# A hybrid decoder block on one core: V and output gate of the linear attention in one product, accumulators kept in one set of pools, and the order of the last norms

## The chip, the cores and the metric

The kernel runs on one core of a Trainium2 chip. The metric is the device time in microseconds, the median over runs; before the change it is 1220.12 us (three runs, 1219.98 to 1223.33). Beside the runs there is one profiled execution, from which all rows below come.

## The reference

One layer over 512 tokens of width 1024, batch 1, all float32:

```
h = rms_norm(x, g0);  proj = h @ w_in                       # 10816 columns
y_a = rglru_mixer(lru_x, lru_g, ...)                        # conv of width 4, gates, linear recurrence
y_b = nsa_mixer(q, kv, gate, ...)                           # compressed, selected and window attention
y_c = gla_mixer(q, k, v, og, lr, ...)                       # 4 heads, keys of 128, values of 256, chunks of 32
merged = sum_i sigmoid(merge_i) * (y_i @ w_branch[i])
x = x + rms_norm(merged @ w_out, g1)
h = rms_norm(x, g2);  gt, up = split(h @ w_ffn_in)
x = x + rms_norm((silu(gt) * up) @ w_ffn_out, g3)
```

In `gla_mixer` each head does `o = causal(q_t k_t^T) v + q_t state`, the state runs over the sequence, and the output is `rms_norm(o) * silu(og)`.

## The kernel before

Every large product is made of three matmuls of two-part operands: each weight piece (128 partitions x 1024 values, from one or two transfers into `wraw`) is split into a high part `whi` (ACT casts, line 91) and a low part `wlo` (DVE or POOL subtracts, line 92), the activations are held as `hh` and `hl`, and high x high, high x low and low x high add up in one accumulator. `wraw`, `whi` and `wlo` have three buffers each. From the attention's end on the pieces are a list, in the order of their use, and `take` (line 815) splits two pieces ahead of the one that it hands out.

The program's stages, in order: first norm; the small projection and the compressed blocks (to about 95 us); the attention, with the other projections fed in between its parts (to 321); four LRU blocks (to 466); four heads of the linear attention (to 640); the merge (to 806); w_out and two norms (to 870); FFN's first product (to 1101); FFN's second product, last norm and store.

Up to the attention the framework's scheduler orders the work, by its own estimate of times. In the stages under `manual_schedule`, among them the attention, the LRU, the linear attention, the merge, and FFN's second product, each engine's queue is in the order in which the code issues it, so an instruction that waits holds up all behind it on its engine. Transfers of weights are issued from SP's queue, the sums that prepare FFN's second product from POOL's.

PSUM has eight banks. The attention uses four pools: `pg` (1), `pa` (4), `pt` (2), `po` (1). At its end these close and new ones open: `pg` with four banks, `pa` with two, `pt` with two. At FFN's second product they close again, and eight accumulators take all banks.

A head of the linear attention (line 1163) issues: the product for q and k (`stream_t`: weights stationary, 512 columns moving, two accumulators); `gla_qk` on DVE, which reads both accumulators and scales q and k by the decays; the transposes of the head before (`gla_turn`); V's product (`stream_tok`: activations stationary, 256 columns of weights moving, four row blocks in two accumulators); `gla_scores`; the output gate's product in the same form, and after it the exponentials for the next head; `gla_out` with the state (three products, three DVE operations), the Silu of the gate, the output, its squares and the root. `lru_params` (line 893) loads `wr`, splits it on ACT and DVE and computes the LRU's constants; it is issued ahead of the first LRU block. The last block's `lru_root` and `lru_scan` stand ahead of the first head.

FFN's second product is a product of 2 x 2 blocks with seven products p1 to p7 in place of eight. Its first loop makes p2, p5, p3 and p1 over eleven slices, then p4, p6 and p7 follow, each with five full weight pieces and a half one. `gain` squares half a row on ACT with its sum and multiplies it with the norm's weights on DVE in place, so the multiply waits for the square; `mean` and `root` make the row's factor, `store` multiplies, adds the residual and sends it off.

## Time and profile before

| | us |
|---|---|
| runs, median (lowest to highest) | 1220.12 (1219.98 to 1223.33) |
| profiled execution | 1221.34 |
| its span, first to last instruction | 1219.6 |
| TensorE busy | 1197.8 (98%) |
| DVE busy | 656.9 (54%) |
| ACT busy | 550.7 (45%) |
| POOL busy | 202.9 (17%) |

Busy time is the time in which an engine has at least one instruction under way. Matmuls overlap, so a recorded duration is longer than the time that a matmul takes from the next one. The view of waits lists for an engine who ended its idle times.

### The profile page before, as it was taken

Reading aid. Unit: us, or ns where it says so; the run is one execution under the profiler, and the core shown is the slowest. Engines: PE = TensorE matmul, PEld = TensorE weight load, DVE = VectorE, ACT = ScalarE, POOL = GpSimd, SP = SyncE. Lnnn points to the kernel's source line nnn. Section 1 sums busy time; section 2 is a strip of 40 time slices with the busy share of each in tenths; the row PEclk is TensorE's granted clock in tenths of the full one; section 3 lists DMA queues with packets and bytes.
Section 4 is the critical chain, followed back from the end, with each engine's and each line's share of the span. In section 5 each row is a group of like instructions: output and inputs, shape, how many; then the busy total and the mean of one; then the engine's idle time right before and its main releaser. Section 6 shows DMA issues by size and latency. Waiting matters only on the chain.

```text
span 1219.6 us, 18072 instructions
## 1 busy us (share of the span) xinstructions
PE 1197.8 (98%) x6834; PEld 1011.7 (83%) x6834; DVE 656.9 (54%) x1308; ACT 550.7 (45%) x1038; POOL 202.9 (17%) x261
## 2 busy tenths in 40 slices
PE   8999999999999999999999999999999999999995
PEld 7897888888788888999998888887988888887884
DVE  5615555555576779465543353446543433446786
ACT  5326556655387676443442233234432323324553
POOL 1224555665101113112221000000000000000000
PEclk8999999999999999999999999999999999999999
DMA  7831422221234547476669334244333333324652
GB/s 248 237 86 29 96 74 66 66 66 53 64 109 130 166 123 228 150 177 145 138 134 207 104 99 160 87 155 138 95 113 87 103 91 100 104 82 159 212 182 91
DMA packets 162102, 151.04 MB, mean 124 GB/s; under 512 B 26706, under 2 KB 139582, under 8 KB 161840
## 3 DMA queue, kind: packets, MB, share of 16 engines
q1 hardware_dynamic: 154912, 125.77, 34.9%
q0 software_dynamic: 6512, 23.07, 8.4%
q8 instruction: 54, 0.88, 0.3%
q10 hardware_dynamic: 592, 1.05, 0.2%
q14 instruction: 32, 0.26, 0.1%
HBM read 145.60 MB, written 27.34 MB: 142 GB/s over the span
## 4 chain that ended last, share of the span: by engine, by line
PE 92%; DVE 4%; ACT 2%; DMA 1%; issue 1%; SPq 0%; DVEq 0%; ACTq 0%
PE gps L836 17%; PE gps L164 14%; PE gps L839 9%; PE gps L122 8%; PE gps L123 7%; PE gps L124 7%; PE gps L167 7%; PE ops L668 4%; PE s L600 3%; PE ptp L646 3%; PE acc L123 3%; PE acc L122 3%; PE acc L124 3%; PE hid L434 1%; PE ops L1125 1%
## 5 line engine op out<-in xcount | busy, mean ns | idle before, releaser
L91 ACT CAST whi<-wraw 128x1024 fp32r<-128x1024 f32 x153 | 159.6, 1049 | 252.2 <-issue 100.7
L92 DVE TENSOR_TENSOR wlo<-wraw,whi 128x1024 fp32r<-128x1024 f32 x131 | 159.9, 1228 | 149.9 <-ACT whi L91 117.9
L164 PE MATMUL gps<-hh,whi 128*128 128x512 f32 x368 | 143.5, 390 | 0.0
L167 PE MATMUL gps<-hl,whi 128*128 128x512 f32 x368 | 143.4, 390 | 0.0
L836 PE MATMUL gps<-hh,whi 128*128 128x512 f32 x320 | 125.4, 392 | 1.6 <-ACT whi L91 1.6
L839 PE MATMUL gps<-hl,whi 128*128 128x512 f32 x320 | 124.6, 389 | 0.0
L122 PE MATMUL gps<-whi,hh 128*128 128x256 f32 x320 | 92.4, 289 | 0.0
L123 PE MATMUL gps<-wlo,hh 128*128 128x256 f32 x320 | 90.6, 283 | 1.4 <-DVE wlo L92 1.4
L164 PE MATMUL gps<-hh,wlo 128*128 128x512 f32 x368 | 90.9, 389 | 0.0
L124 PE MATMUL gps<-whi,hl 128*128 128x256 f32 x320 | 90.5, 283 | 0.0
L164 PEld LDWEIGHTS gps<-hh,whi 128*128 128x128 f32 x368 | 69.1, 188 | 15.0 <-issue 0.9
L167 PEld LDWEIGHTS gps<-hl,whi 128*128 128x128 f32 x368 | 69.1, 188 | 14.5 <-issue 0.2
L164 PEld LDWEIGHTS gps<-hh,wlo 128*128 128x128 f32 x368 | 69.1, 188 | 14.4
L650 DVE COPY psb<-ptp 128x512 f32<-128x512 f32 (+2 forms) x72 | 45.5, 631 | 65.3 <-PE ptp L646 61.6
L611 ACT ACTIVATE p<-p,mx 128x384 f32<-128x384 f32 (+3 forms) x128 | 68.7, 538 | 26.0 <-DVE mx L609 25.9
L836 PE MATMUL gps<-hh,wlo 128*128 128x512 f32 x320 | 79.1, 389 | 0.0
L625 POOL TENSOR_TENSOR p<-p,sc 128x256 f32<-128x256 f32 (+3 forms) x64 | 75.5, 1201 | 1.9
L808 POOL COPY tick<-whi 128x1 f32<-128x1 f32 x44 | 28.0, 636 | 284.2 <-ACT whi L91 284.1
L836 PE MATMUL gps<-yh,whi 128*128 128x512 f32 x192 | 74.8, 390 | 0.0
L839 PE MATMUL gps<-yl,whi 128*128 128x512 f32 x192 | 74.7, 389 | 0.0
L122 PE MATMUL gps<-hh,whi 128*128 128x512 f32 (+1 forms) x176 | 73.8, 420 | 0.1
L836 PEld LDWEIGHTS gps<-hh,whi 128*128 128x128 f32 x320 | 60.1, 188 | 14.5 <-ACT whi L91 2.0
(362 smaller groups left out, 2556.6 us busy)
## 6 DMA issues: line engine op xcount, KB each, us to landing
wraw<-in_w_in_dram SPq DMA_DIRECT2D x60, 512.0 KB, 4.1
wraw<-in_w_ffn_in_dram SPq DMA_DIRECT2D x88, 256.0 KB, 3.2
rows_d<-in_w_ffn_out_dram POOLq DMA_DIRECT2D x22, 512.0 KB, 5.2
cols_d<-in_w_ffn_out_dram POOLq DMA_DIRECT2D x22, 512.0 KB, 6.5
wraw<-in_w_in_dram SPq DMA_DIRECT2D x32, 256.0 KB, 4.1
wraw<-in_w_branch_dram SPq DMA_DIRECT2D x16, 512.0 KB, 3.4
wraw<-in_w_ffn_out_dram SPq DMA_DIRECT2D x18, 256.0 KB, 3.5
bias<-line_d SPq DMA_DIRECT2D x16, 256.0 KB, 4.5
```

The costliest lines, as they stand in the source:

```text
L91: a_.copy(hi, raw)
L92: lo_eng.tensor_tensor(lo, raw, f(hi), op=OP.subtract)
L122: pe.matmul(ps, lh, rh, start=first, stop=False)
L123: pe.matmul(ps, lh, rl, start=False, stop=False)
L124: pe.matmul(ps, ll, rh, start=False, stop=last)
L164: pe.matmul(ps[n], part_[:, k, c], ah[:, kk], start=kk == 0 and part_ is h, stop=kk == 7 and part_ is l)
L167: pe.matmul(ps[n], h[:, k, c], al[:, kk], start=False, stop=False)
L611: a_.activation(o, o, AF.Exp, scale=-1.0, bias=mx[:, br, gi:gi + 1], accum_out=sm[:, br, gi:gi + 1])
L625: g_.tensor_tensor(o, o, sc[:, br][:, :, None].to_broadcast([128, 2, n]), op=OP.mult)
L668: pe.matmul(ops[h, qb * 128:qb * 128 + 128], v, m, start=first and i == 0, stop=last and i == len(blocks) - 1)
L836: pe.matmul(ps[n], part_[:, k, c], ah[:, kk], start=kk == 0 and part_ is h, stop=kk == 7 and part_ is l)
L839: pe.matmul(ps[n], h[:, k, c], al[:, kk], start=False, stop=False)
```

## The change

Eight things are changed.

1. The product of V and the product of the output gate of one head become one product of 512 columns (`stream_vog` with pieces from `vog_pieces`: 256 rows of 256 + 256 columns, two transfers each, four pieces a head as before). It has four accumulators, one for each row block of 128 tokens; for the first two pieces two row blocks go first and then the other two. V is copied and the gate's Silu taken from these accumulators, by row block.
2. State and output of a head move into the next one: `gla_state` and the next head's exponentials stand between the two halves of the next q/k product, `gla_out` and `gla_gate` behind `gla_qk`, `gla_turn` behind the third piece of the next V and gate product. For the last head these places are in the merge's first chunk. `qs` gets a second buffer.
3. The last LRU block's `lru_root` and `lru_scan` stand between the halves of the first q/k product, the constants and the first exponentials behind it.
4. `lru_params` goes from ahead of the first LRU block to behind its gate products; the transfer of `wr` stays ahead.
5. In `small_proj` the reversed copy, four small products and the gates' sigmoid go ahead of the low-rank part.
6. The attention's PSUM pools stay to the end: `Banks` hands out the four banks of the old `pa` as the new `pg`, and those of `pg` and `po` in turn as the new `pa`. FFN's second product takes its eight accumulators from them.
7. In FFN's second product the additions of p1 come two pieces later, the gains of the second halves of blocks 0 and 1 move from p4 into p6, `gain` writes to another tile for one half of each block, the last half-width weight piece is loaded and split during p6 into a place of its own, and roots and stores of the last blocks are issued in another order.
8. A Sqrt of one constant column is issued on ACT behind the last FFN chunk.

The diff, cut to its core:

```diff
+        gps = pt.tile([128, TB, 64], F32, name="gtps", tag="pt")
+        srev = pp.tile([128, TB, 128], F32, name="srev", tag="psb", bufs=NPSB)
+        v_.tensor_copy(srev, sps.rearrange("p (b c) -> p b c", b=TB)[:, :, ::-1])
+        for tb in range(TB):
+            pe.matmul(gps[:, tb], srev[:, tb], ii, start=True, stop=True)
+        a_.activation(gates, gps[:, :, 16:64], AF.Sigmoid)
...
-        gps = pt.tile([128, TB, 64], F32, name="gtps", tag="pt")
-        srev = pp.tile([128, TB, 128], F32, name="srev", tag="psb", bufs=NPSB)
-        v_.tensor_copy(srev, sps.rearrange("p (b c) -> p b c", b=TB)[:, :, ::-1])
-        for tb in range(TB):
-            pe.matmul(gps[:, tb], srev[:, tb], ii, start=True, stop=True)
-        a_.activation(gates, gps[:, :, 16:64], AF.Sigmoid)
...
-    psum_ctx.close()
-    psum_ctx = ExitStack()
-    pg = psum_ctx.enter_context(tc.tile_pool(name="pg2", bufs=4, space=PSUM))
+    class Banks:
+        def __init__(self, *pools):
+            self.pools, self.i = pools, -1
+        def tile(self, shape, dt, name, tag):
+            self.i += 1
+            p, t = self.pools[self.i % len(self.pools)]
+            return p.tile(shape, dt, name=name, tag=t)
+    pg, pa = Banks((pa, "a")), Banks((pg, "g"), (po, "o"))
     gpools = [(pg, "g"), (pg, "g")]
-    pa = psum_ctx.enter_context(tc.tile_pool(name="pa2", bufs=2, space=PSUM))
-    pt = psum_ctx.enter_context(tc.tile_pool(name="pt2", bufs=2, space=PSUM))
...
+    def vog_pieces(h):
+        def load(p):
+            aps = [(lambda t, n=n: t.rearrange("p (k c) -> p k c", k=2)[:, :, n * 256:n * 256 + 256],
+                    dap(w_in, p * 256 * INW + c + h * 256, [[INW, 128], [128 * INW, 2], [1, 256]]))
+                   for n, c in enumerate((GLA_V, GLA_OG))]
+            return [t.rearrange("p (k c) -> p k c", k=2) for t in split_w(load_raw(aps), lo_eng())]
+        return [lambda p=p: load(p) for p in range(4)]
...
-        pieces += in_pieces([(GLA_V + h * 256, 256)]) + in_pieces([(GLA_OG + h * 256, 256)])
+        pieces += vog_pieces(h)
...
-    def stream_tok(act, *after):
-        ps = [p.tile([128, 2, 256], F32, name="gps", tag=t) for p, t in gpools]
-        both = [ps[tb // 2][:, tb % 2] for tb in range(TB)]
-        for kh in range(2):
-            for _ in steps_tok(both, take(), kh, act):
-                pass
-            if kh < len(after) and after[kh]:
-                after[kh]()
+    def stream_vog(act, *after):
+        ps = [pg.tile([128, S], F32, name="gps", tag="g") for _ in range(TB)]
+        ah, al = act
+        got = []
+        for p, tbs in ((0, (0, 1)), (1, (0, 1)), (0, (2, 3)), (1, (2, 3)), (2, range(TB)), (3, range(TB))):
+            if p == len(got):
+                got.append(take())
+            h, l = got[p]
+            for tb in tbs:
+                t = slice(tb * 128, tb * 128 + 128)
+                for kk in range(2):
+                    k = 2 * p + kk
+                    mm3(ps[tb], ah[:, k, t], al[:, k, t], h[:, kk], l[:, kk], k == 0, k == 7)
+            if TB - 1 in tbs and p < len(after) and after[p]:
+                after[p]()
         return ps
...
+    sy.dma_start(wr, gla_wa2[0])
     def lru_params():
-        sy.dma_start(wr, gla_wa2[0])
...
-    lru_params()
...
+        if cp == 0:
+            lru_params()
...
-    lru_root()
-    lru_scan(3)
+    pq = stream_t(hT, chain(lru_root, lambda: lru_scan(3)))
...
-        QS = gp_.tile([128, 4, 4, CH], F32, name="qs")
+        QS = gp_.tile([128, 4, 4, CH], F32, name="qs", bufs=2)
...
-    def gla_out(at, QS, KST, V, sfx, psg):
-        atf = at.rearrange("p b n c -> p b (n c)")
+    def gla_state(KST, V, sfx):
...
+        return ST
+    def gla_out(at, QS, ST, V):
...
-        for b2 in range(2):
-            a_.activation(sg[:, 2 * b2:2 * b2 + 2], psg[b2], AF.Silu)
...
-    held = []
+    G_ = {}
+    gla_consts()
+    Z["x"] = gla_exp(0)
+    def gla_next():
+        G_["st"] = gla_state(G_["kst"], G_["v"], G_["sfx"])
+        if G_["h"] < 3:
+            Z["x"] = gla_exp(G_["h"] + 1)
     for h in range(4):
-        pq = stream_t(hT, gla_consts if h == 0 else None, (lambda: Z.update(x=gla_exp(0))) if h == 0 else None)
+        if h:
+            pq = stream_t(hT, gla_next)
         e_ = Z["x"]
         QT, QS, KS, sfx = gla_qk(*pq, *e_)
-        if held:
-            gla_turn(h - 1, held.pop())
-        V = gp_.tile([128, TB, 256], F32, name="gv")
+        if h:
+            yt = gla_gate(*gla_out(AT[(h - 1) % 2], G_["qs"], G_["st"], G_["v"]), G_["sg"])
         if h == 1:
             new_y(ya)
         sp = [(lambda k=k: y_split(k)) if h == 1 else None for k in range(4)]
-        pv = stream_tok(hT, sp[0], sp[1])
-        for b2 in range(2):
-            a_.copy(V[:, 2 * b2:2 * b2 + 2], pv[b2])
+        if h:
+            sp[2] = chain(*([sp[2]] if sp[2] else []), lambda: gla_turn(h - 1, yt))
+        pv = stream_vog(hT, *sp)
+        V = gp_.tile([128, TB, 256], F32, name="gv")
+        sg = gp_.tile([128, TB, 256], F32, name="gsg")
+        for tb in range(TB):
+            a_.copy(V[:, tb], pv[tb][:, 0:256])
+        for tb in range(TB):
+            a_.activation(sg[:, tb], pv[tb][:, 256:512], AF.Silu)
         KST = gla_scores(AT[h % 2], QT, KS, *e_[1:])
-        pog = stream_tok(hT, sp[2], chain(*([sp[3]] if sp[3] else []), *([lambda: Z.update(x=gla_exp(h + 1))] if h < 3 else [])))
-        held.append(gla_gate(*gla_out(AT[h % 2], QS, KST, V, sfx, pog)))
...
+            first = c == 0 and i == 0
...
-                pg_ = stream_t(hT)
+                pg_ = stream_t(hT, gla_next if first else None)
...
-            if c == 0 and i == 0:
-                gla_turn(3, held.pop())
...
+            if first:
+                yt = gla_gate(*gla_out(AT[1], G_["qs"], G_["st"], G_["v"]), G_["sg"])
...
+            if first:
+                gla_turn(3, yt)
+                gctx.close()
+                mtp = mtc.enter_context(tc.tile_pool(name="mtp", bufs=1, side="right"))
+                mT.extend(mtp.tile([128, 8, S], F32R, name=n) for n in ("mth", "mtl"))
...
+    stream.pop()
...
+        a_.activation(cst[:, 2:3], cst[:, 0:1], AF.Sqrt)
...
             c = C[tb][:, hf * 512:hf * 512 + 512]
-            jk = fp.tile([128, 512], F32, name="fjk", tag="fsg", bufs=2)
+            o = gained[tb, hf] = fp.tile([128, 512], F32, name="fsg", bufs=2) if (hf == 0) == (tb < 2) else c
+            jk = half("fjk", 8 + hf)
             a_.activation(jk, c, AF.Square, accum_out=ssf[:, tb, hf:hf + 1])
-            v_.tensor_tensor(c, c, gb3[:, hf * 512:hf * 512 + 512], op=OP.mult)
+            v_.tensor_tensor(o, c, gb3[:, hf * 512:hf * 512 + 512], op=OP.mult)
...
-                        a_.copy(C[2 + tt][:, c0], p2[tt])
-                    for tt in range(2):
-                        a_.copy(C[tt][:, c0], p5[tt])
-                w = weights()
-                use(p3, LS1[k], 3, w, 0, k)
...
-            for p in range(NP):
-                w = weights()
-                for k in range(2 * p, min(2 * p + 2, NK)):
-                    use(p4, LS2[k], 2, w, k % 2, k)
-                if p == 0:
-                    second(NK - 1)
-                if p in (0, 1):
-                    add(C[p][:, c1], p3[p], C[p][:, c0])
-                    add(C[2 + p][:, c1], p3[p], C[2 + p][:, c0], OP.subtract)
-                    add(C[p][:, c0], p1[p], C[p][:, c0], OP.subtract)
-                    add(C[2 + p][:, c1], p1[p], C[2 + p][:, c1])
-                if p in (2, 3):
-                    gain(p - 2, 1)
-                if p == 4:
...
-                        sy.dma_start(x_, x1_d[:, i // 2, i % 2 * 512:i % 2 * 512 + 512])
-            for p in range(NP):
-                w = weights()
-                for k in range(2 * p, min(2 * p + 2, NK)):
-                    use(p6, LS2[k], 0, w, k % 2, k)
-                if p in (0, 1):
-                    add(C[2 + p][:, c0], p4[p], C[2 + p][:, c0])
-                    gain(2 + p, 0)
-                if p in (2, 3):
-                    add(C[p - 2][:, c0], p4[p - 2], C[p - 2][:, c0])
-            for p in range(NP - 3):
-                w = weights()
-                for k in range(2 * p, 2 * p + 2):
-                    use(p7, LS2[k], 1, w, k % 2, k)
-                if p in (0, 1):
-                    add(C[2 + p][:, c1], p6[p], C[2 + p][:, c1])
-                    gain(2 + p, 1)
-                    mean(2 + p)
-                if p == 1:
+        def add(o, x_, y, op=OP.add):
+            v_.tensor_tensor(o, x_, y, op=op)
+        p2, p5 = [[p.tile([128, 512], F32, name="acc", tag=n) for _ in range(2)] for p, n in ((pa, "a"), (pt, "pt"))]
+        p3, p1 = [[pg.tile([128, 512], F32, name="acc", tag="g") for _ in range(2)] for _ in range(2)]
+        p4, p6, p7 = p2, p5, p3
...
+        for p in range(NP):
+            w = weights()
+            for k in range(2 * p, min(2 * p + 2, NK)):
+                use(p4, LS2[k], 2, w, k % 2, k)
+            if p == 0:
+                second(NK - 1)
+            if p in (0, 1):
+                add(C[p][:, c1], p3[p], C[p][:, c0])
+                add(C[2 + p][:, c1], p3[p], C[2 + p][:, c0], OP.subtract)
+            if p in (2, 3):
+                add(C[p - 2][:, c0], p1[p - 2], C[p - 2][:, c0], OP.subtract)
+                add(C[p][:, c1], p1[p - 2], C[p][:, c1])
...
+        lastw = []
+        for p in range(NP):
+            w = weights()
+            for k in range(2 * p, min(2 * p + 2, NK)):
+                use(p6, LS2[k], 0, w, k % 2, k)
+            if p in (0, 1):
+                add(C[2 + p][:, c0], p4[p], C[2 + p][:, c0])
+                gain(2 + p, 0)
+            if p in (2, 3):
+                add(C[p - 2][:, c0], p4[p - 2], C[p - 2][:, c0])
+                gain(p - 2, 1)
+            if p == 3:
+                raw = raw_tile()
+                sy.dma_start(raw[:, 0:512], cols_d[(2 * NK - 1) * 128:2 * NK * 128])
+            if p == 4:
+                lastw = [HP[0][:, 0, i].rearrange("p a t -> p (a t)") for i in range(2)]
+                a_.copy(lastw[0][:, :512], raw[:, :512])
+                v_.tensor_tensor(lastw[1][:, :512], raw[:, :512], f(lastw[0][:, :512]), op=OP.subtract)
+        w5 = []
+        for p in range(NP - 3):
+            w = weights()
+            for k in range(2 * p, 2 * p + 2):
+                use(p7, LS2[k], 1, w, k % 2, k)
+            if p in (0, 1):
+                add(C[2 + p][:, c1], p6[p], C[2 + p][:, c1])
+                if p:
                     root(2)
-                if p == 2:
-                    store(2, 0)
-                    store(2, 1)
-                    root(3)
-            w3 = [weights() for _ in range(3)]
-            for tt in range(2):
-                for k in range(2 * NP - 6, NK):
-                    use(p7, LS2[k], 1, w3[(k - 2 * NP + 6) // 2], k % 2, k, (tt,))
-                if tt == 0:
-                    store(3, 0)
-                    store(3, 1)
-                add(C[tt][:, c0], p7[tt], C[tt][:, c0])
-                if tt == 1:
-                    root(0)
-                gain(tt, 0)
-                mean(tt)
-            store(0, 0)
-            store(0, 1)
-            root(1)
-            store(1, 0)
-            store(1, 1)
+                gain(2 + p, 1)
+                mean(2 + p)
+            if p == 2:
+                store(2, 0)
+                store(2, 1)
+                root(3)
+                store(3, 0)
+                store(3, 1)
+        w3 = [weights() for _ in range(2)] + [lastw]
+        for tt in range(2):
+            for k in range(2 * NP - 6, NK):
+                use(p7, LS2[k], 1, w3[(k - 2 * NP + 6) // 2], k % 2, k, (tt,))
+            add(C[tt][:, c0], p7[tt], C[tt][:, c0])
+            gain(tt, 0)
+            mean(tt)
+            if tt == 0:
+                root(0)
+                store(0, 0)
+        store(0, 1)
+        root(1)
+        store(1, 0)
+        store(1, 1)
+        psum_ctx.close()
```

## Rows read from the trace of the kernel before

**Rows 1.** The page: the span, TensorE's busy time with its share and count, and the clock granted to TensorE in 40 equal slices (tenths of full speed).

```profile
span 1219.6 us, 18072 instructions
...
PE 1197.8 (98%) x6834; PEld 1011.7 (83%) x6834; DVE 656.9 (54%) x1308; ACT 550.7 (45%) x1038; POOL 202.9 (17%) x261
...
PEclk8999999999999999999999999999999999999999
```

**Rows 2.** The view of waits, TensorE alone: the waiting group, whom it waited for, then the total in us, how often, and the longest.

```profile
PE acc L122 <- ACT whi L1433: 1.9, 2, 1.5
PE gps L836 <- ACT whi L91: 1.6, 1, 1.6
PE gps L123 <- DVE wlo L92: 1.4, 1, 1.4
...
PE acc L123 <- DVE wlo L1434: 1.1, 2, 0.8
PE acc L122 <- DVE am L1407: 0.8, 1, 0.8
PE gtps L381 <- DVE srev L379: 0.8, 1, 0.8
```

**Rows 3.** TensorE's timeline in the second head of the linear attention: start in us, duration, line, operation, output and operands, shape, count. The first two rows are the first and the last of 40 matmuls of OG's product in a row; then the first row of the state and the first of the q/k product behind state and output; then the first of the scores and the first of OG's product behind them.

```profile
499.81 0.28 PE L124 MATMUL gps<-whi,hl 128*128 128x256 f32 x1
...
504.49 0.28 PE L124 MATMUL gps<-whi,hl 128*128 128x256 f32 x1
504.61 1.46 PE L1110 MATMUL kvps<-gv,kst 128*128 128x256 f32 x6
...
508.74 0.58 PE L836 MATMUL gps<-hh,whi 128*128 128x512 f32 x1
...
532.24 1.05 PE L1083 MATMUL atps<-qt,en 128*128 128x128 f32 x8
...
534.83 0.41 PE L122 MATMUL gps<-whi,hh 128*128 128x256 f32 x1
```

**Rows 4.** The chain of waits: start, duration, what. The two rows are the state's products of the first and of the third head, two heads apart.

```profile
504.77 1.29 PE kvps L1110 x6
...
588.42 1.29 PE kvps L1110 x6
```

**Rows 5.** TensorE's timeline in two other stretches of 512-column matmuls in the order high x high, high x low, low x high. The first pair is from w_out's product (33 distances lie between the two), the second from FFN's second product (9 distances).

```profile
824.14 0.39 PE L124 MATMUL gps<-woh,mtl 128*128 128x512 f32 x1
...
831.84 0.40 PE L124 MATMUL gps<-woh,mtl 128*128 128x512 f32 x1
...
1174.70 0.39 PE L122 MATMUL acc<-whi,hh 128*128 128x512 f32 x1
...
1176.74 0.39 PE L122 MATMUL acc<-whi,ls 128*128 128x512 f32 x1
```

**Rows 6.** DVE's timeline around the first head: the LRU's last product (its two scans and a multiply follow), the split of V's first piece, and in the head the first and third operation of gla_qk and the split behind it.

```profile
472.83 1.23 DVE L981 TENSOR_TENSOR ii__4926<-ii__4926,a 128x1024 f32<-128x1024 f32 x1
...
477.61 1.22 DVE L92 TENSOR_TENSOR wlo<-wraw,whi 128x1024 fp32r<-128x1024 f32 x1
...
480.72 0.68 DVE L1057 SCALAR_TENSOR_TENSOR qt<-gps,eb 128x512 f32<-128x512 f32 x1
...
481.92 0.68 DVE L1061 TENSOR_TENSOR ee<-gps,ee 128x512 f32<-128x512 f32 x1
...
484.97 2.35 DVE L92 TENSOR_TENSOR wlo<-wraw,whi 128x1024 fp32r<-128x1024 f32 x2
```

**Rows 7.** The timelines of ACT and DVE at the end of the attention: ACT's last copy for it, DVE's first memset of lru_params, ACT's two casts of wr, and ACT's next three weight splits. In brackets: idle time before, and what ended it.

```profile
313.93 0.59 ACT L650 COPY psb<-ptp 128x512 f32<-128x512 f32 x1
...
316.43 0.48 DVE L895 MEMSET wa<- 128x512 f32 x1
...
317.65 1.26 ACT L897 CAST wa<-wr 16x512 fp32r<-16x512 f32 x2 [3.13 <-DMA wr<-in_gla_wa_dram]
...
321.79 2.93 ACT L91 CAST whi<-wraw 128x1024 fp32r<-128x1024 f32 x3
```

**Rows 8.** ACT's, DVE's and TensorE's timelines in the first two LRU blocks: a table load of ACT and the instruction after it, DVE's two operations that make xl of the second block, and the product of TensorE that reads xl.

```profile
346.37 1.28 ACT L958 ACT_TABLE_LOAD   x1
347.67 0.69 ACT L958 ACTIVATE rr<-rips,par 128x512 f32<-128x512 f32 x1
...
373.87 1.52 DVE L937 TENSOR_TENSOR xl<-xc,xh 128x512 fp32r<-128x512 f32 x2
...
380.42 0.40 PE L123 MATMUL rips<-xl,gwh 128*128 128x512 f32 x1
```

**Rows 9.** DVE's timeline in small_proj: the operation that stands ahead of the reversed copy.

```profile
93.97 0.67 DVE L372 TENSOR_TENSOR lr<-lr,sps 16x512 f32<-16x512 f32 x1
```

**Rows 10.** ACT's and DVE's timelines at the end of the program: the table load for the first root, DVE's split of the last full weight piece, the last but one gain's multiply with the idle time before it, and the last multiplies.

```profile
1194.91 1.28 ACT L1522 ACT_TABLE_LOAD   x1
...
1202.20 1.23 DVE L1434 TENSOR_TENSOR wlo<-am,whi 128x1024 fp32r<-128x1024 f32 x1 [0.54 <-ACT whi L1433]
...
1208.85 0.69 DVE L1515 TENSOR_TENSOR hl<-hl,gb 128x512 f32<-128x512 f32 x1 [0.85 <-ACT fjk L1514]
...
1214.91 1.42 DVE L1536 SCALAR_TENSOR_TENSOR hl<-hl,rs_r,xr 128x512 f32<-128x512 f32 x2
```

**Rows 11.** ACT's timeline in the second head: one read of 256 columns of an accumulator.

```profile
507.40 0.38 ACT L1129 ACTIVATE gjk<-ops 128x256 f32<-128x256 f32 x1 [1.99 <-PE ops L1127]
```

67 lines of the change are left out of this document (33 added, 34 removed).

## The prediction

> **What bounds the kernel now.** I read the page's totals first. TensorE has a matmul in flight for 1197.8 of 1219.6 us and its granted clock is at the upper of its two levels from the second slice on [rows 1]. So an edit counts only where it ends a wait of TensorE or takes column time off it. The view of waits, for TensorE alone, comes next: it names a handful of single waits [rows 2], each of which the diff touches, and nothing that repeats. A matmul's recorded duration is its latency, not its cost, because the next one starts before it ends: the 256-column matmuls of V and OG last 0.28 us each, but 39 of them lie between 499.81 and 504.49, which is 120 ns from start to start [rows 3]. I therefore work with distances between starts. One head of the linear attention repeats every 41.8 us [rows 4]: 48 matmuls of 512 columns, 192 of 256 columns (23.0 us), and small float32 products for the rest.
>
> **The change part by part.** The sum is made against the profiled execution: 1221.34 us, its span of 1219.6 and 1.7 around it. The median of the runs is 1220.12, so what I find is taken off that median.
>
> *V and OG in one 512-column product.* Per head 192 matmuls at 120 ns become 96. The trace has no such stretch in the linear attention, but two near ones. In w_out's product (stationary activations, moving weights, six in a row into one bank, just as in the new loop) 33 distances take 7.70 us, 233 ns each. Where FFN's second product reads its stationary operand from the memory that holds hh here, 9 distances take 2.04 us, 227 ns [rows 5]. That gives 22.4 or 21.8 us for 23.0: 0.6 or 1.25 us a head, 2.6 or 5.0 in four. The order of the instructions is w_out's and the place of the operands is FFN's, so I take 230 ns: 22.1 us a head, **-3.8 us**, bounds -5.0 and -2.5.
> The Trainium skill ("TensorE: Matmul & The Clock Gate", Back-to-back issue gap) gives an isolated warm matmul N/2.4 + 2.5 ns, so 109 ns for 256 columns and 216 for 512. By that rule the merge would bring an estimated 0.25 us a head, 1.0 in all; the rows, at 120 and 227, carry about 13 ns over the columns in both forms, and so speak for more.
>
> *State, output and turn moved into the next head.* The same float32 products are issued, in four groups per head instead of three. A switch back costs nearly nothing: of a head's 41.8 us [rows 4] 10.9 are the q/k product (48 x 227 ns), 23.0 are V and OG, 4.1 state and output (504.61 to 508.74) and 2.6 the scores (532.24 to 534.83) [rows 3], so the turn's eight transposes and all three switches share 1.2 us. I take **+0.2** for four switches more; at most 0.3 each, 1.2. A gain is excluded, as TensorE waits nowhere in a head [rows 2]. Nothing waits behind the moved products: the turn needs DVE's work of gla_qk (480.72 to 485.0 [rows 6]), then output, root and four multiplies, by my estimate some 9 us after the q/k product, and comes 19 us after it.
>
> *First head.* TensorE waits 1.4 us for the low half of V's first weight piece [rows 2], because DVE did the LRU's last product, scans and multiply from 472.83 before starting that split at 477.61 [rows 6]. In the new order the first split stands ahead of these 4.8 us and the second behind them, ending at about 479.9. V starts at 477.1 (the old split's end at 478.8, less the wait and the one matmul before it); the new loop needs the second piece 12 matmuls later, 477.1 + 2.8 = 479.9. So the wait shrinks to about nothing: **-1.4**. Late next are two banks: the third row block takes the bank of q, the fourth that of k, which DVE frees by lines 1057 to 1061 (480.72 to 482.6 before [rows 6], about the same after). They are needed from 482.7 on. If the exponentials slip, up to 1.7 comes back: bounds -1.6 and +0.3.
>
> *End of attention.* ACT waits for the transfer of wr (its two casts start at 317.65), then for DVE, loads a table and does the logarithm, and only then splits three weight pieces from 321.79 [rows 7], for which TensorE waits 1.6 us [rows 2]. With lru_params gone from there the first split can run when ACT's last copy for the attention is done, at 314.5 [rows 7], seven us earlier; the other two need buffers that TensorE leaves only during its last chunk, but are wanted later. I take **-1.6**; bounds -2.0 with the restart, and -1.0 if DVE's low half comes late.
>
> *lru_params put into the first LRU block.* It takes ACT and DVE from the memset at 316.43 to the next split at 321.79, less 0.6 spent on the transfer: 4.8 us [rows 7], and now two more table loads of 1.28 [rows 8], one of them beside DVE's part. Queued behind it on ACT are the next splits, the tanh and exponentials, and through them DVE's scan and convolution of the second block. Its xl ends at 375.4, and TensorE's second gate product needs it at 380.42 [rows 8]: 5.0 us of cover against 4.8 plus 1.3, and the block before no longer starts with three splits in one lump (2.93 us at 321.79 [rows 7]), for which I count about 0.8. I take **+0.3**, bounds 0 and +2.8.
> A table load is followed by the next ACT instruction 1.30 us after its start (346.37 to 347.67) [rows 8]. The Trainium skill ("ScalarE: Activation LUTs", What ACT_TABLE_LOAD costs) adds a drain of 1.38 us to each; by it the two loads would cost an estimated 2.8 more here, which the row doesn't bear out.
>
> *Small orders at the start.* DVE does the sum of line 372 (0.67) before the reversed copy of line 379, for which TensorE waits 0.8 [rows 2, 9]. The copy now comes first: **-0.8**, bounds -1.1 and 0, since this stretch isn't written out by hand and its scheduler may place the copy elsewhere.
>
> *PSUM pools kept.* The only wait that I see them cause is at FFN's second product: 0.8 us for the last chunk's multiply [rows 2], and by my estimate 0.2 for the restart. The first accumulators then lie in banks that have been idle since the linear attention, so this goes: **-1.0**, at least -0.3. Late next is nothing, as the third and fourth accumulators come 2.7 and 4 us later.
>
> *FFN's end.* TensorE waits 1.9 + 1.1 us for late splits [rows 2] ; then DVE works from 1202.2 to 1216.3, almost without a pause, to the last multiply at 1214.91 [rows 10]. DVE is what ends last, so the waits themselves are worth little. Off DVE's end go the half-width split (0.6) and one wait of 0.85 for ACT's square, before the multiply at 1208.85 [rows 10], since the gained row goes to another tile; in the last block root(0) fills that wait already. Against it, two gains with such waits move into the product before, where they delay the next three splits by about as much as the earlier table load (1.28, at 1194.91 before) gives back. I take **-1.0**, bounds -2.5 and +0.7 (nothing saved, one gain's 1.5 us half exposed).
>
> Sum: -3.8 + 0.2 - 1.4 - 1.6 + 0.3 - 0.8 - 1.0 - 1.0 = -9.1 us. In the profiled execution that is 1212.2, against the median **1211.0**.
>
> **Rivals.**
> (a) *The bank hand-off.* V and OG fill all four accumulators, and the next q/k product may start only when ACT has copied V and done the first Silu. If ACT did all four copies and two Silus after the last matmul, that is 6 x 0.38 (a 256-column read of an accumulator [rows 11]) + 1.28 for the table + 0.1 = 3.7 us, against 2.6 us of scores: 1.1 us a head, 4.4 in all, 1215.4. Against it: the row blocks end 1.4 us apart, so only the last copy waits and the first Silu ends 2.2 us after the product.
> (b) *Moved work turns up late elsewhere.* lru_params delays the second LRU block by its upper bound, and the gains moved in FFN's end bring that to its own: 2.5 + 1.7 more, 1215.2.
> (c) *The merge saves nothing.* If a 512-column matmul comes to cost as much as two of 256, 240 ns, columns alone count and the term of 3.8 falls away: 1214.8. Against it stand the 227 and 233 ns of rows 5. The Trainium skill's formula above is near this case, with an estimated 1213.8.
> (d) *Slower.* The 512-column stretches at 227 ns fall into w_out's 233 ns. Both spacings occur at the same granted clock and operand shape [rows 5], so something in order or placement sets it, and the change moves the banks. By the loops in the code LRU, linear attention, merge and FFN hold 32 + 21 calls of 48 such matmuls and 462 in the second product, 3000; 6.6 ns each is 20 us, 1231. It decides from 9.1 / 0.0066 = 1400 matmuls on. Against it: the order of instructions in those loops stays as it is, and the weights' and activations' places too.
> (e) *The change doesn't do what it says:* the pools and moves leave TensorE's waits as they are and only the merge counts: -3.6, 1216.5.
>
> **Chances.** Forecast 0.66, (a) 0.09, (b) 0.11, (c) 0.05, (d) 0.05, (e) 0.04. The median's 0.3% is 3.7 us, about what a measurement of this kernel can tell from no change: the limit lies at 1216.5. The forecast's own range is 1207 to 1214.5; (a), (b) and (c) reach up to 1217 with their spread, and all lower bounds together give 13.0 us, 1207.1, less a little for the spread of the runs. So 1206.5 to 1217. About half of (e) and a third of (a) and (b) fall within 0.3%: faster 0.86, same 0.09, slower 0.05.
>
> **What would show it.** Right: no wait of TensorE at the LRU's first product, at V's first low half, at FFN's second product and at gtps; a head's period near 40.9 us; 512-column matmuls 227 to 233 ns apart in V and OG. Wrong: a wait at the second block's gate products over 1 us; a wait of the q/k product for Silu in each head; the last multiply no earlier after FFN's start than before. A period above 41.5 us would refute the largest term.

## The result and the profile after

The changed kernel takes 1206.69 us (median of five runs, 1206.61 to 1206.77) against 1220.12 (five runs of the kernel before in the same call, 1219.22 to 1223.33). The ratio is 0.9885, 95% interval 0.987 to 0.9899. That is 13.4 us less where 9.1 were forecast. The median lies 0.2 inside the range (1206.5 to 1217); the ratio, which pairs runs, puts the time at 0.9885 x 1220.12 = 1206.1, just below it. The profiled execution took 1206.69, with a span of 1204.8. One run of the kernel before in a later call took 2965.31 us, in a slow state of the chip, and is left out of the medians below.

The page of the kernel after (span, the engines' busy time, and the clock granted to TensorE in 40 slices):

```profile
span 1204.8 us, 17332 instructions
...
PE 1188.2 (99%) x6450; PEld 988.8 (82%) x6450; DVE 656.5 (54%) x1308; ACT 554.9 (46%) x1058; POOL 208.8 (17%) x261
...
PEclk9999999999999999999999999999999999999999
```

TensorE has 384 matmuls fewer (192 became 96 in each of four heads) and is busy 9.6 us less; the other 5.2 us of the span were idle time. DVE and POOL issue as many instructions as before, ACT 20 more (4.2 us), among them the reads of V and gate by row block. Against [rows 1] the first slice of the clock is a 9, not an 8: this belongs to the result, as will be seen.

The view of waits of the kernel after, TensorE alone:

```profile
PE acc L123 <- DVE wlo L1477: 0.8, 1, 0.8
PE acc L122 <- ACT whi L1476: 0.5, 1, 0.5
PE rips L123 <- DVE xl L963: 0.4, 1, 0.4
```

The six rows of [rows 2] were one wait at the LRU's first product, one at V's low half, one at gtps, one at FFN's second product and four at its end. Only two at FFN's end are left, 0.5 and 0.8; the row of the LRU's gate product was there before. No row names the q/k product, so the accumulators are handed on in time.

Where the difference arises is read by laying the same instruction of both timelines side by side. TensorE's timeline before, at the boundaries of the stages (start, duration, line, operation, operands; in brackets idle time and who ended it):

```profile
16.93 0.41 PE L123 MATMUL gps<-hl,whi 128*128 128x512 f32 x1
...
95.29 0.32 PE L381 MATMUL gtps<-ii,srev 128*128 128x64 f32 x1 [0.84 <-DVE srev L379]
...
322.87 0.50 PE L836 MATMUL gps<-hh,whi 128*128 128x512 f32 x1 [1.57 <-ACT whi L91]
...
383.87 0.39 PE L836 MATMUL gps<-yh,whi 128*128 128x512 f32 x1
...
657.75 0.39 PE L839 MATMUL gps<-hl,whi 128*128 128x512 f32 x1
...
1101.11 0.50 PE L122 MATMUL acc<-whi,ls 128*128 128x512 f32 x1 [0.85 <-DVE am L1407]
...
1209.92 0.39 PE L124 MATMUL acc<-whi,hh 128*128 128x512 f32 x1
```

The same in the kernel after:

```profile
15.01 0.40 PE L123 MATMUL gps<-hl,whi 128*128 128x512 f32 x1
...
92.05 0.32 PE L373 MATMUL gtps<-ii,srev 128*128 128x64 f32 x1
...
318.17 0.39 PE L853 MATMUL gps<-hh,whi 128*128 128x512 f32 x1
...
378.96 0.39 PE L853 MATMUL gps<-yh,whi 128*128 128x512 f32 x1
...
646.28 0.39 PE L856 MATMUL gps<-hl,whi 128*128 128x512 f32 x1
...
1088.63 0.39 PE L122 MATMUL acc<-whi,ls 128*128 128x512 f32 x1
...
1194.99 0.39 PE L124 MATMUL acc<-hh 128*128 128x512 f32 x1
```

The lead grows as follows; the last column is the step from row to row.

| up to | lead, us | step |
|---|---|---|
| the second matmul of the first projection (16.93 / 15.01) | 1.92 | 1.92, before any changed line |
| gtps (95.29 / 92.05) | 3.24 | 1.32; 0.28 of it is order alone, as gtps now stands ahead of some of the attention's products instead of behind them |
| the LRU's first product (322.87 / 318.17) | 4.70 | 1.46, so 1.74 behind what gtps left |
| a product in the second LRU block, behind its gate products (383.87 / 378.96) | 4.91 | 0.21 |
| the merge's first chunk (657.75 / 646.28) | 11.47 | 6.56 |
| FFN's second product (1101.11 / 1088.63) | 12.48 | 1.01 |
| the last matmul (1209.92 / 1194.99) | 14.93 | 2.45 |
| the end of the span (1219.6 / 1204.8) | 14.8 | -0.1 |

Between the merge and FFN's second product nothing but that one wait changed: 443.36 us before, 442.35 after. So the products of 512 columns kept their spacing.

DVE's timeline after, its split of the last full weight piece and its last multiply (before: [rows 10]):

```profile
1188.55 1.23 DVE L1477 TENSOR_TENSOR wlo<-am,whi 128x1024 fp32r<-128x1024 f32 x1 [1.21 <-ACT whi L1476]
...
1200.73 0.74 DVE L1586 SCALAR_TENSOR_TENSOR hl<-hl,rs_r,xr 128x512 f32<-128x512 f32 x1
```

### The profile page after: what moved, and what is told of

Its sections match the earlier page's. It is cut to its first block, busy times and chain, and to the rows that moved or that the text cites. A ratio compares the mean times of both kernels' runs of the same rounds, so it can differ in the third digit from the quotient of the medians.

```text
span 1204.8 us, 17332 instructions
## 1 busy us (share of the span) xinstructions
PE 1188.2 (99%) x6450; PEld 988.8 (82%) x6450; DVE 656.5 (54%) x1308; ACT 554.9 (46%) x1058; POOL 208.8 (17%) x261
## 3 DMA queue, kind: packets, MB, share of 16 engines
q10 hardware_dynamic: 592, 1.05, 0.2%
## 4 chain that ended last, share of the span: by engine, by line
PE 94%; DVE 3%; ACT 1%; issue 1%; DMA 0%; SPq 0%; DVEq 0%; ACTq 0%
PE gps L853 19%; PE gps L164 14%; PE gps L856 9%; PE gps L122 8%; PE gps L123 7%; PE gps L124 7%; PE gps L167 7%; PE ops L668 4%; PE s L600 3%; PE ptp L646 3%; PE acc L123 2%; PE acc L124 2%; PE acc L122 2%; PE hid L434 1%; PE ops L1151 1%
## 5 line engine op out<-in xcount | busy, mean ns | idle before, releaser
L167 PEld LDWEIGHTS gps<-hl,whi 128*128 128x128 f32 x368 | 69.1, 188 | 14.5 <-issue 0.2
L825 POOL COPY tick<-whi 128x1 f32<-128x1 f32 x44 | 33.8, 768 | 271.7 <-ACT whi L91 271.7
L164 PEld LDWEIGHTS gps<-hh,wlo 128*128 128x128 f32 x368 | 69.1, 188 | 14.3
L853 PEld LDWEIGHTS gps<-hh,wlo 128*128 128x128 f32 x320 | 60.1, 188 | 12.5
L856 PEld LDWEIGHTS gps<-hl,whi 128*128 128x128 f32 x320 | 60.1, 188 | 12.3
L122 PE MATMUL gps<-whi,hh 128*128 128x512 f32 (+1 forms) x192 | 69.9, 364 | 0.0
```

The lines of the kernel that those rows point to most:

```text
L122: pe.matmul(ps, lh, rh, start=first, stop=False)
L164: pe.matmul(ps[n], part_[:, k, c], ah[:, kk], start=kk == 0 and part_ is h, stop=kk == 7 and part_ is l)
L167: pe.matmul(ps[n], h[:, k, c], al[:, kk], start=False, stop=False)
L853: pe.matmul(ps[n], part_[:, k, c], ah[:, kk], start=kk == 0 and part_ is h, stop=kk == 7 and part_ is l)
L856: pe.matmul(ps[n], h[:, k, c], al[:, kk], start=False, stop=False)
```

## The experiments

Each kernel is one edit away from the kernel after, if nothing else is said; "runs" are its times beside those of the kernel before in the same call.

**The kernel before, again.** No edit.

> The kernel before, unchanged. In the profile after, TensorE's first 128-column products fall from 215 to 106 ns at 5.6 us, in the profile before only at about 16.3 us, and 1.9 us of the 14.9 us between the two spans lie there, though the code of this stretch is the same. If that is a chance of the execution, the runs of this kernel show both cases: some with a span near 1217.7 and others near 1219.6 us. If the change causes it, all runs stand at 1219.6 and a mean granted clock of 0.995.

Measured: 12 runs, median 1222.14, from 1220.29 to 1224.43; 17 runs of the kernel before beside them, 1219.3 to 1223.75. The execution of 1219.3 had a span of 1217.6 and a mean granted clock of 0.998; the one of 1224.43 had 1222.7 and 0.991. So the same program differs by 5 us, and the clock goes with it. The profile taken here (span 1222.6) shows where; windows of this execution, with busy time and count of each engine, then the granted clock:

```profile
95.00:97.00 2.00, 2.00 (x13) 1.66 (x12) 1.88 (x14) 1.47 (x2) 0.00 (x0) 0.71 0.00 0
97.00:99.00 2.00, 2.00 (x6) 1.57 (x5) 0.00 (x0) 1.99 (x12) 0.00 (x0) 0.50 0.00 0
...
1204.00:1207.00 3.00, 2.62 (x7) 1.50 (x8) 2.90 (x8) 0.62 (x1) 0.00 (x0) 0.70 0.45 175
1207.00:1210.00 3.00, 3.00 (x8) 2.33 (x8) 2.15 (x4) 0.72 (x2) 0.00 (x0) 0.50 0.45 175
```

The same windows of the first profile of this kernel:

```profile
97.00:99.00 2.00, 2.00 (x9) 1.62 (x10) 0.87 (x12) 1.99 (x6) 0.00 (x0) 1.00 0.00 0
...
1207.00:1210.00 3.00, 3.00 (x15) 2.38 (x13) 1.91 (x5) 0.90 (x3) 0.00 (x0) 1.00 0.45 175
```

In three microseconds at the lower level TensorE starts 8 matmuls instead of 15. Both stretches lie shortly behind waits that the change takes away or shortens: gtps and the last splits. Against the first profile they cost 1.5 us behind gtps and 2.5 at the end. In the first profile the clock was at the lower level somewhere else, in the transposes of the first norm behind an idle time of 1.88 us (10.88 to 16.3). So neither rival of the expectation holds as stated: it is a chance of the execution, but one that happens behind some of the waits.

**V and OG as two halves.**

```diff
-                    mm3(ps[tb], ah[:, k, t], al[:, k, t], h[:, kk], l[:, kk], k == 0, k == 7)
+                    for cs in (slice(0, 256), slice(256, 512)):
+                        mm3(ps[tb][:, cs], ah[:, k, t], al[:, k, t], h[:, kk][:, cs], l[:, kk][:, cs], k == 0 and cs.start == 0, k == 7 and cs.start > 0)
```

> The kernel after, each 512-column matmul of V and OG issued as two of 256 columns. If the merge gains by the distance between starts (120 ns twice against 230), a head's period goes from 40.6 to about 41.6 us and the time from 1206.7 to about 1210.6. If the gain in the heads comes from the moved work or from fewer switches, the time stays at 1206.7.

Measured: 1212.53 (1211.98 to 1212.65), 5.8 above the kernel after; the span is 5.3 longer, 0.5 of which arises at the start. The chain of waits of the kernel after (start, duration; the state's products of the first and the last head, three periods apart):

```profile
502.31 1.30 PE kvps L1134 x6
...
624.16 1.30 PE kvps L1134 x6
```

The same with two halves:

```profile
503.99 1.30 PE kvps L1135 x6
...
629.50 1.30 PE kvps L1135 x6
```

A period of 40.62 against 41.84 us, and 41.83 before [rows 4]. All of a head's gain, 1.2 us, is the width of the matmul; the moved state and output by themselves brought and cost nothing. The spacing is read from TensorE's timeline after: the first two products of a stretch behind state and output, and its last, 70 distances further:

```profile
511.74 0.58 PE L122 MATMUL gps<-whi,hh 128*128 128x512 f32 x1
512.16 0.40 PE L123 MATMUL gps<-wlo,hh 128*128 128x512 f32 x1
...
528.06 0.39 PE L124 MATMUL gps<-whi,hl 128*128 128x512 f32 x1
```

The first distance is 0.42 us, the restart behind other products. The 70 behind it take 15.90 us, 227 ns each and not the 230 of the forecast; only with the first one taken in is the average 230. In the kernel with halves 18 distances (559.81 to 561.97) give 120 ns. Two times 120 less 227, 96 times a head, is 1.25 us. V and OG stand in two stretches a head in all three kernels, so the number of edges is the same: the first distances of these are 0.20 and 0.25 us before, 0.31 and 0.21 with halves, 0.42 and 0.32 after. From edge to edge both products of a head take 23.23 us before, 23.30 with halves and 22.11 after. The Trainium skill's formula for an isolated matmul ("TensorE: Matmul & The Clock Gate", Back-to-back issue gap) gives 109 and 216 ns, and from these an estimated gain of 1.0 us in all. Measured were four times 1.2, so here the rows decide against it.

**State and output left in their own head.** `gla_state`, `gla_out` and `gla_gate` stand directly behind `gla_scores`, `gla_exp` for the next head ahead of them.

```diff
-            pq = stream_t(hT, gla_next)
+            pq = stream_t(hT)
...
-            yt = gla_gate(*gla_out(AT[(h - 1) % 2], G_["qs"], G_["st"], G_["v"]), G_["sg"])
...
         KST = gla_scores(AT[h % 2], QT, KS, *e_[1:])
-        G_.update(h=h, kst=KST, v=V, sfx=sfx, qs=QS, sg=sg)
+        if h < 3:
+            Z["x"] = gla_exp(h + 1)
+        yt = gla_gate(*gla_out(AT[h % 2], QS, gla_state(KST, V, sfx), V), sg)
```

> The kernel after, with state, output and gate of a head issued right behind its scores, not in the next head. DVE ends the copy of the turned keys 1.7 us after the last score product, and the state's sums take DVE 1.5 us more before the output can end: if the move is what makes the merge possible without a wait, TensorE waits about 2 to 3 us a head, 1215 to 1219 in all. If the scores (2.6 us) cover it, the time stays at 1206.7.

Measured: 1214.17 (1213.5 to 1215.59); the span is 7.0 longer. The waits, TensorE alone:

```profile
PE kvps L1134 <- DVE kst L1127: 6.4, 4, 1.6
```

TensorE waits 1.6 us in each head for DVE's copy of the turned keys, and some 0.2 us more are lost behind it: the chain puts a period at (625.51 - 498.31) / 3 = 42.4 us, 1.78 longer. The second half of the expectation did not come: the output's products hide the sums of the state. So the move is what the merge needs: with OG's product gone from between the scores and the state, something else has to stand there.

**No Sqrt behind the last FFN chunk.**

```diff
-        a_.activation(cst[:, 2:3], cst[:, 0:1], AF.Sqrt)
         HP += ...
```

> The kernel after without the Sqrt of a constant column behind the last FFN chunk, so that ACT loads the table for the first root of the last norm, in the third product from the end. If the table load stood in front of the late splits and these set the end, the time goes up by 1.1 to 1.3, to about 1207.9. If DVE's queue sets the end alone, or the load falls into slack, it stays at 1206.7.

Measured: 1207.42 (1207.14 to 1208.98); the span is 1.0 longer. ACT's timeline:

```profile
1182.24 1.28 ACT L1571 ACT_TABLE_LOAD   x1
1183.53 0.20 ACT L1571 ACTIVATE rs_r<-rs_m 128x1 f32<-128x1 f32 x1
1183.64 1.03 ACT L1476 CAST whi<-am 128x1024 fp32r<-128x1024 f32 x1
```

The table load stands ahead of a weight split and delays it; TensorE's wait for the last full piece grows from 0.5 to 1.4, and its clock is at a mean of 0.60 from 1192 to 1195 us (1.00 in the kernel after). The instruction behind the load starts 1.29 us after it, so a load costs its own duration and no drain is seen. The Trainium skill ("ScalarE: Activation LUTs", What ACT_TABLE_LOAD costs) adds a drain of 1.38 us, by which this kernel would be an estimated 2.4 slower instead of 1.0.

**Four parts taken back, one at a time.** The reversed copy in `small_proj` behind the low-rank part; `lru_root` and `lru_scan(3)` ahead of the first q/k product; `lru_params` ahead of the first LRU block; a new pool of eight accumulators at FFN's second product.

```diff
-        gps = pt.tile([128, TB, 64], F32, name="gtps", tag="pt")
...
         v_.tensor_tensor(smallT[64:80], lr, f(smallT[0:16]), op=OP.subtract)
+        gps = pt.tile([128, TB, 64], F32, name="gtps", tag="pt")
...
```

> The kernel after, with the reversed copy and its four products in small_proj back behind the low-rank part. If only the wait comes back, all runs stand 0.8 to 1.1 us above the kernel after, at 1207.6 to 1207.8, and near each other. If a wait here can also be followed by a stretch at the lower clock, as in the second profile of the kernel before (96.5 to 98.6 us, 1.2 us in all), the runs fall into two groups, near 1207.7 and near 1209.

```diff
-    pq = stream_t(hT, chain(lru_root, lambda: lru_scan(3)))
+    lru_root()
+    lru_scan(3)
+    pq = stream_t(hT)
```

> The kernel after, with the last block's lru_root and lru_scan ahead of the first q/k product again. If DVE's 4.8 us ahead of the first split of V and OG is what made TensorE wait, the wait of 1.4 to 1.6 us comes back, 1208.2. If the two-piece order of the new loop or the earlier splits hide it, the time stays at 1206.7.

```diff
+    lru_params()
     for cp in range(4):
...
-        if cp == 0:
-            lru_params()
```

> The kernel after, with lru_params ahead of the first LRU block again. If ACT's chain at the attention's end was the cause of the 1.7 us wait, it comes back and the time is about 1208.4; the place in the first LRU block, where it stands now, cost nothing. If moving it cost something in the second LRU block, less than that is lost, 1207 to 1208.

```diff
+        psum_ctx.close()
+        fa = psum_ctx.enter_context(tc.tile_pool(name="facc", bufs=1, space=PSUM))
+        acc = [fa.tile([128, 512], F32, name=f"acc{i}") for i in range(8)]
+        p3, p1, p2, p5 = [acc[2 * i:2 * i + 2] for i in range(4)]
```

> The kernel after, with the PSUM pools closed ahead of FFN's second product and one pool of eight accumulators opened, as before. If the wait at that product (0.85 us and the restart) comes from the pool, the time is 1207.7. If the wait came from the order of ACT and DVE there, it stays at 1206.7.

Each brings back the one row of waits that it should, and no other. In the same order, each from the view of waits of its own kernel:

```profile
PE gtps L381 <- DVE srev L379: 0.8, 1, 0.8
```

```profile
PE gps L123 <- DVE wlo L92: 1.3, 1, 1.3
```

```profile
PE gps L853 <- ACT whi L91: 1.5, 1, 1.5
```

```profile
PE acc L122 <- DVE am L1450: 0.8, 1, 0.8
```

| kernel | its span over that of the kernel after | runs: median (lowest to highest) |
|---|---|---|
| gtps_late | 1.4 (0.4 of it at the start) | 1209.13 (1207.54 to 1210.93) |
| lru_root_early | 1.7 | 1208.60 (1208.09 to 1209.19) |
| lru_params_early | 2.0 | 1208.88 (1208.41 to 1209.76) |
| pools_reopen | 1.0 (0.2 less at the start) | 1208.36 (1207.67 to 1209.43) |

The wait and the restart behind it (0.2 to 0.5 us more) make up the span. The runs of gtps_late fall into two groups, 1207.5 and 1208.0 at a mean clock of 0.997 and 0.996, and 1210.3 and 1210.9 at 0.995. That fits a lower clock behind the wait in the second pair, as in the second profile of the kernel before. But the second pair lies some 2.9 us above the first, more than the 1.5 lost there, the profile taken here keeps the clock at 1.00 behind gtps, and these two runs have no trace: the cause is not shown.

**The kernel after, again.** No edit.

> The kernel after, unchanged, on the chip of the other runs. If the scatter of the kernel before (1219.3 to 1224.4) comes from stretches at the lower clock behind waits of TensorE that are gone in this kernel, its runs stand close together at 1206.6 to 1207. If the scatter is that of the chip or of the start, it spreads over 2 us or more here as well.

Measured: 1207.28 (1206.62 to 1207.59), on a chip on which the kernel before had a median of 1223.12. The five runs of the result and the four here span 1.0 us; the kernel before spans over 5. What is left in this profile lies at the start. Few runs show this: gains_p4 and late_mean below, whose waits past the start are no longer, spread over 1.7 and 2.3 us. Windows of this execution:

```profile
10.00:12.00 2.00, 1.42 (x7) 1.42 (x8) 1.89 (x7) 1.46 (x5) 0.00 (x0) 0.53 1.09 387
12.00:14.00 2.00, 2.00 (x13) 2.00 (x12) 1.89 (x5) 0.00 (x0) 0.00 (x0) 0.62 1.09 360
```

**The last half piece in the stream again.** `stream.pop()`, the separate load and `lastw` are taken out; `w3` takes three pieces from the stream.

```diff
-    stream.pop()
...
-        w3 = [weights() for _ in range(2)] + [lastw]
+        w3 = [weights() for _ in range(3)]
```

> The kernel after, with the last half-width weight piece split in the stream again, behind the second last. By the prediction's step DVE's chain to the end gets the 0.69 us of that split back, and TensorE two waits of about 0.5: 1207.4. If the split fell into slack of DVE, 1206.7; if a stretch at the lower clock follows the waits, some runs at 1209.

Measured: 1210.93 (1210.24 to 1211.65), more than any of the three cases gave. ACT's timeline (ACTq: a transfer that ACT issues):

```profile
1187.37 1.03 ACT L1476 CAST whi<-am 128x1024 fp32r<-128x1024 f32 x1
1190.35 2.50 ACTq L1586 DMA_DIRECT2D out_dram<-hl  x2
1192.95 0.62 ACT L1476 CAST whi<-am 128x512 fp32r<-128x512 f32 x1 [4.55 <-DVE hl L1585]
```

The cast of the half piece stands on ACT behind the transfers of two finished row halves, and the second of these waits until DVE has made it. So TensorE waits 2.5 us for the cast, and the clock is at 0.50 in the six us behind it (1193 to 1199). So with the new order of the stores the old place of the split costs 4.3 us of the span.

**The gains back in p4.** p1's additions in p4's first two pieces, the gains of the second halves of blocks 0 and 1 in the third and fourth.

```diff
             if p in (0, 1):
...
+                add(C[p][:, c0], p1[p], C[p][:, c0], OP.subtract)
+                add(C[2 + p][:, c1], p1[p], C[2 + p][:, c1])
             if p in (2, 3):
-                add(C[p - 2][:, c0], p1[p - 2], C[p - 2][:, c0], OP.subtract)
-                add(C[p][:, c1], p1[p - 2], C[p][:, c1])
+                gain(p - 2, 1)
```

> The kernel after, with p1's additions in the first two pieces of p4 and the gains of the second halves of blocks 0 and 1 in the third and fourth, as before. The prediction counted the moved gains as a cost that takes back the 1.28 us of the earlier table load: then this version is faster, near 1205.5. If the moved gains cost nothing, it stays at 1206.7; if they were moved because p4 has no room, it is slower.

Measured: 1206.55 (1206.36 to 1208.07). The span is 1.4 longer and all of it is at the start (a low clock there); from 16 us on the two kernels run at the same distance. The moved gains cost nothing.

**The gained row in place.**

```diff
-            o = gained[tb, hf] = fp.tile([128, 512], F32, name="fsg", bufs=2) if (hf == 0) == (tb < 2) else c
+            o = gained[tb, hf] = c
```

> The kernel after, with every gained row written in place, so that the multiply waits for ACT's square, as before. By the prediction's step one wait of 0.85 us comes back on DVE's last chain: 1207.5. If both of the last two gains wait, 1208.4. If the chain has slack there, 1206.7.

Measured: 1209.58 (1208.79 to 1210.57); the span is 2.1 longer. DVE's timeline, the last two gains:

```profile
1195.54 0.69 DVE L1565 TENSOR_TENSOR hl<-hl,gb 128x512 f32<-128x512 f32 x1 [0.79 <-ACT fjk L1564]
...
1199.79 0.69 DVE L1565 TENSOR_TENSOR hl<-hl,gb 128x512 f32<-128x512 f32 x1 [0.85 <-ACT fjk L1564]
```

Both of the last gains wait for ACT's square, and one earlier puts off the last full split by 0.9. The clock is at 0.50 from 1192 to 1195 us in this profile. In the order of the kernel after no root stands where it could fill the last of these waits.

**mean(3) behind the last full split.** Built on what the trace of the kernel after shows at its end.

```diff
                 gain(2 + p, 1)
-                mean(2 + p)
+                if p == 0:
+                    mean(2)
             if p == 2:
+                mean(3)
                 store(2, 0)
```

> The kernel after, with mean(3), whose root waits on ACT for DVE, issued behind the split of the last full piece. In the trace after ACT's cast of that piece starts 0.1 us behind this root (1187.49), though ACT was idle before it. If the root holds the cast and through it TensorE (0.67 and 1.03 us of waits) and DVE's last chain, the chain ends 0.7 to 0.9 us earlier: 1205.9. If the cast waits for its buffer or its transfer, nothing changes, 1206.7, or mean(3) is late and it gets slower.

Measured: 1206.05 (1205.94 to 1208.22), against 1207.28 for the kernel after in the same call; the span is 1204.0, 0.8 shorter. ACT's timeline after (the root that waits for DVE, then the cast):

```profile
1187.38 0.20 ACT L1572 ACTIVATE rs_r<-rs_m 128x1 f32<-128x1 f32 x1 [0.78 <-DVE rs_m L1571]
1187.49 1.03 ACT L1476 CAST whi<-am 128x1024 fp32r<-128x1024 f32 x1
```

And in this kernel:

```profile
1186.35 0.19 ACT L1564 ACTIVATION_READ_ACCUMULATOR fjk<-hl 128x1 f32 x1
1186.44 1.04 ACT L1476 CAST whi<-am 128x1024 fp32r<-128x1024 f32 x1
```

The cast starts 1.05 us earlier, the wait of 0.5 is gone and that of 0.8 is 0.6. This version is ahead of the kernel after by 0.8 in the profiles (0.15 of it at the start) and by 0.7 from lowest to lowest run; one of its four runs, 1208.22, is slower than all of that kernel.

**Two stores on ACT and POOL.** On top of late_mean, the second halves of blocks 2 and 3 are scaled on ACT and added on POOL.

> The kernel late_mean, with the second halves of the stores of blocks 2 and 3 scaled on ACT and added on POOL instead of on DVE. If DVE's queue alone sets the end behind the last split, two multiplies of 0.67 us less bring 1.2, to 1204.8. If the last blocks' chain through TensorE's last product sets it, less than 0.5.

Measured: 1205.76 (1205.69 to 1206.34), with the span of late_mean, 1204.0. The first and fastest of the two expectations fails. DVE's timeline while POOL adds (1190.87 to 1193.96):

```profile
1191.81 1.00 DVE L1565 TENSOR_TENSOR fsg<-hl,gb 128x512 f32<-128x512 f32 x1
1192.89 1.09 DVE L1569 TENSOR_TENSOR ss<-ssf 128x1 f32<-128x1 f32 x1
```

These two take 0.69 and 0.16 us when POOL is idle, so 1.24 of the 1.34 us that two multiplies take are lost again. A sum of one column that lasts 1.09 us and ends as POOL ends was held up. The Trainium skill ("SBUF — State Buffer", SBUF: two separate sides) says that DVE with two operands from SBUF and POOL exclude one another for a whole instruction; this row agrees. Whether the chain through TensorE's last product would otherwise have set the end, as the second expectation has it, is not shown.

**The start filled.**

```diff
+                for i in range(10 if tb == 1 else 0):
+                    pe.matmul(tps[i % 8][:, 128:256], wz, wz, start=True, stop=True)
                 for ft in range(8):
                     pe.transpose(...)
```

> The kernel after, with ten more products of the zero tile (128 columns, results overwritten) between the first and the second row block of the first transposes, where TensorE idles 1.1 to 2.3 us for x and in some profiles (the second one of the kernel after, 10.8 to 13.2 us) then runs at the lower clock. If the idle time is what the lower clock follows, all runs stand at 1206.6 to 1206.8. If the clock falls there for another reason, the runs still spread to 1207.6.

> The kernel late_mean with the ten products of start_fill. If both hold by themselves, 1205.9 in all runs, faster than the kernel after by 0.7 and than the kernel before by 14 to 17.

Measured: start_fill 1206.58 (1206.44 to 1206.68), mean_and_fill 1206.36 (1205.97 to 1207.12). The clock stays up in both profiles; windows of start_fill:

```profile
10.00:12.00 2.00, 2.00 (x21) 2.00 (x20) 1.79 (x8) 1.14 (x2) 0.00 (x0) 1.00 1.09 386
12.00:14.00 2.00, 1.86 (x17) 1.52 (x15) 1.99 (x3) 0.87 (x2) 0.01 (x1) 1.00 1.09 356
```

But mean_and_fill spreads over 1.2 us all the same. In its profile the first projection starts at 15.70 us, in that of start_fill at 14.66. ACT's timelines show why, at the squares of the second row block; the first row is of mean_and_fill, the second of start_fill:

```profile
8.23 1.06 ACT L278 ACTIVATE jk<-xt 128x1024 f32<-128x1024 f32 x1 [1.28 <-DMA xt<-in_x_dram]
...
7.20 1.06 ACT L278 ACTIVATE jk<-xt 128x1024 f32<-128x1024 f32 x1
```

So the start varies also with the arrival of x, and the ten products win no time that could be told from none.

## Why the prediction was right or wrong

**Direction, places and order of size were right.** Each wait named in [rows 2] that was to go is gone, and the four that hang on a part of their own come back alone when it is undone. The merge is the largest term. None of the five rivals came: no wait of the q/k product (a); the second LRU block's gate products come 4.9 us earlier than before, the first block's first product 4.7, so nothing is delayed between them (b); 512 columns start 227 ns apart, not 240 (c); the long products keep their spacing, 442.35 us from the merge to FFN's second product against 443.36 with the wait (d); and the parts that are not the merge bring 8 of 12.8 us (e).

**The sum was too small, for three reasons.** At a mean clock of 0.998 the kernel before has a span of 1217.6 and the kernel after one of 1204.8. So about 12.8 us are work and waits, where the steps gave 9.1; the rest of the medians' difference, 0.6 in this call and up to 3.0 in others, I put down to the clock and the start, which only the profiled executions show.

- *V and OG, and the switches: -3.8 and +0.2 forecast, four times 1.2 = -4.8 measured.* The mechanism was right and a size was off. The step that failed is "The order of the instructions is w_out's and the place of the operands is FFN's, so I take 230 ns": the new products start 227 ns apart, as in FFN's second product, so the term is 192 x 120 - 96 x 227 ns = 1.25 us a head, -5.0 in four, which is its bound. w_out's 233 ns do not come with the order of the instructions, which the new loop shares; what sets them stays open. Between -5.0 and the measured -4.8 lie the 0.2 forecast for four switches more.
- *FFN's end: -1.0 forecast, -2.4 measured.* The step that failed is "two gains with such waits move into the product before, where they delay the next three splits by about as much as the earlier table load (1.28, at 1194.91 before) gives back". The table load gives back 1.0 (no_sqrt) and the gains cost nothing (gains_p4), and the last full split starts 1.2 earlier after FFN's second product: 99.92 us behind it, against 101.09 [rows 10]. This 1.2 cannot be shared out: the table load in its old place and the gains in place each put the split off again by 0.8 to 0.9. DVE's work from there to its end takes 12.92 us against 14.13, the other 1.2; half split and one wait were counted there as 1.45, and with the gains in place it takes 14.12 again. The upper end of the gain, 2.5, held it. The undone parts cost 4.3, 2.1 and 1.0, more than the whole gain: in the new order each has become a condition for the others.
- *The stretch that ends with the merge's first chunk: -1.4 forecast beside the heads, -1.7 measured,* and the attention's end with the first LRU block and the second's gate products: -1.3 forecast, -1.95 measured. Here each wait was counted as the view of waits gives it, with 0 to 0.2 for the restart; a whole wait is worth 0.1 to 0.3 more than that. lru_params was charged 0.3 in its new place, and no loss is seen behind it: the lead goes from 4.70 to 4.91.

**What the prediction left out altogether is the clock.** [Rows 1] showed an 8 in the first slice and the sum took it for something that stays. In the profiled executions 1.9 us of the lead are there, before any changed line: that much of the profile's difference is no effect of the change. But the median can gain by it too: behind gtps and the last splits the kernel before loses 1.5 and 2.5 us in its second profile and nothing in its first, and these waits are gone or shorter.

gtps (-0.8 forecast, -1.04 measured) and FFN's second product (-1.0 forecast, -1.01 measured) came out as worked.

What stays open: why the clock falls behind a wait in one execution and not in another, and whether the wait is the cause. In the profiles of this study an idle time of 1.27 us at the start (lru_root_early) left the clock up, 1.33 (gtps_late) and 1.69 (after_again) had it fall, and 1.62 (vog_halves) did not. At FFN's end waits of 1.5, 0.8, 0.4 and 0.3 us left it up in one profile of the kernel before and not in the other; it fell in no_sqrt, gain_in_place and lastw_stream, where these waits are longer than in the kernel after, and stayed up in the kernel after. Behind the single waits of 1.3 to 1.6 us in the middle of the program, in both profiles of the kernel before, in lru_root_early, lru_params_early and four times in heads_unmoved, it stayed at 1.00. So the length of one wait does not tell it, and no run here settles it.

## What to carry to other kernels

Price a stretch of matmuls by its spacing and its edges apart: 72 products at 230 ns were one distance of 420 and the rest at 227, and an average hides a mis-sized term. Where a trace shows two spacings, forecast with both instead of their middle. A wait of TensorE in a kernel that is otherwise hardly ever idle cost more than its length in every case here: 0.2 to 0.5 us for the restart, and at the start, at gtps and at FFN's end in some executions a stretch at half the clock behind it. Runs that lie far apart can be a sign of such waits. On an engine with an order written out by hand look at what stands ahead of a weight split: a root that waits for another engine, a table load, and a transfer that is issued from the same queue all hold it up.
